# RWKV-7 block inversions for both token halves at once, on 64 partitions

## The chip, the cores and the metric

The kernel runs on one core of one Trainium2 chip. Its time is device microseconds from the first to the last instruction of one launch; the median of the runs counts. The engines of a core are TensorE (PE, with PEld for its weight loads), VectorE (DVE), ScalarE (ACT), GpSimd (POOL) and SyncE (SP). Each works through its own queue in order.

## What is computed

Two layers of a streaming encoder trunk on 512 tokens of width 1024, in float32. Layer 0 mixes tokens with two groups of heads: HGRN2 (four heads of 128) and RWKV-7 (eight heads of 64). Layer 1 mixes with an S5 group and four mLSTM heads. Behind each mixing stand an output projection and a SwiGLU feed-forward part. The change is in RWKV-7 alone:

```python
def step(state, inp):
    r_t, w_t, k_t, v_t, a_t, b_t = inp
    sa = jnp.einsum("bhvk,bhk->bhv", state, a_t)
    state = (state * w_t[:, :, None, :] + sa[..., None] * b_t[:, :, None, :]
             + v_t[..., None] * k_t[:, :, None, :])
    return state, jnp.einsum("bhvk,bhk->bhv", state, r_t)
```

Token by token this would be 512 steps. The kernel works in chunks of 64 tokens instead. Within a chunk each token's `sa` depends on those before it, which is a triangular system I - A of 64 x 64 per head and chunk. Its two diagonal blocks of 32 x 32 are inverted, and the rest is solved with matrix products.

## The kernel before

**Dense products.** A product with weights (`projg`, results in tiles named `d`) takes three TensorE matmuls per 128 x 128 block, because weights and activations are each split into a high and a low part. A product over 1024 features is 24 matmuls of 128 x 512. The split of the weights is a copy on ScalarE (`hi`, L369) and a subtraction (`lo`, L370) on VectorE, for a few units (`pu`) on GpSimd.

**RWKV-7.** Two heads make a pair, so there are pairs 0 to 3, and tokens are taken in two halves g = 0 and 1 of four chunks each. For pairs (2q, 2q+1), q = 0 or 1, there are three stages:

- `rwp(q, g)`: `rw_gates`, then `rw_prep` of both pairs side by side. It builds the matrices of each chunk. The products `r<-ar,bb` are masked into `pb` (L931), and their diagonal blocks go to DRAM (`scr_a`, L943) by DMAs of ScalarE's queue.
- `rw_inverse(q, g)`, written `inv`: GpSimd loads the 32 blocks of q and g from `scr_a` (L973), one block per partition (32 partitions x 1024 elements, tile `iu`), sets the diagonal (L974), and runs 30 steps of a multiply (L978, into `ti`) and an add (L980) in place. It then writes the result to `scr_u` (L982).
- `rwd(q, g)`: `rw_solve` of each pair loads the inverses from `scr_u` into the block-diagonal tile `ub` (L991, GpSimd's queue, four DMAs per pair) and solves with four products: `r<-y,ub`, `r<-z,amb`, `r<-z,ub`, `r<-pb,wu`, with `z` added on VectorE (L1004). Then `rw_chain` of both pairs carries the state from chunk to chunk and normalises the output (`bon`, L1068). The second half's chain needs the state that the first half's left (`hs`).

A pair of index p and p + 2 shares its tiles, and `ub` has one buffer for each of the two pairs of a q. So with q = 0 or 1 and g = 0 or 1 there are four inversions, each of 60 operations on GpSimd.

**HGRN2.** `hgrn(h)` does four dense products and then a head's chain on all engines; some of its subtractions (`e<-c`, L271) are GpSimd's.

**The order.** One stream `F` holds the dense products of the input projection in the order of `seq`: L (small gates), P0, P1 (projections of RWKV-7 pairs 0 and 1), H0 (HGRN2 head 0), P2, P3, H1, H2, H3. The table `prog` lists stages; each weaves a piece of `F`, up to the mark named, with other streams in proportion to costs that they yield (`m` scales them):

1. F to P1
2. `rwp(0,0)`, F to H0
3. `inv(0,0)`, `rwp(0,1)`, F to P2
4. `inv(0,1)`, `rwd(0,0)`, F to H1
5. `rwd(0,1)`, `rwp(1,0)`, F to H2
6. `inv(1,0)`, `rwp(1,1)`, F to H3
7. `inv(1,1)`, `rwd(1,0)`

Behind them `rwd(1,1)`, its costs scaled by 0.2, is woven with the first part of the output projection (`outa`: eight products of 15 matmuls, inputs `ysp`). The second part (L1226: 72 matmuls) needs RWKV-7's pairs 2 and 3 and head 3. A scheduler then orders the instructions of each engine by this order and by what is ready in its own estimate, so products written later can be drawn forward.

Of the kernel before, what the change touches and what calls it, by code (L numbers as in the profile page):

```python
# [10 lines left out]
F32 = mybir.dt.float32  # L11
# [75 lines left out]
def _cols(w, cols):  # L87
    """[K, N] -> [len(cols)/128, 128, K]: per column tile, k tiles side by side."""
    a = w[:, cols]
    k, n = a.shape  # L90
    a = a.reshape(k // P, P, n // P, P)
    return np.ascontiguousarray(a.transpose(2, 1, 0, 3).reshape(n // P, P, k))


def _rows(w, cols, per):
    """[K, N] -> [K/(128 per), 128, per N]: per k tiles side by side, all columns."""
# [6 lines left out]
def _layout(i):  # L103
# [78 lines left out]
    # S5: partitions hold (group of the pair, state), free dims the pair of groups  # L182
# [16 lines left out]
PRM = {'c': (0, 1, 2, 3), 'seq': ['L', 'P0', 'P1', 'H0', 'P2', 'P3', 'H1', 'H2', 'H3'], 'm': {'inv': 1.728, 'rwp': 1.6, 'rwd': 0.675}, 'prog': [[('F', 'P1')], [('rwp', 0, 0), ('F', 'H0')], [('inv', 0, 0), ('rwp', 0, 1), ('F', 'P2')], [('inv', 0, 1), ('rwd', 0, 0), ('F', 'H1')], [('rwd', 0, 1), ('rwp', 1, 0), ('F', 'H2')], [('inv', 1, 0), ('rwp', 1, 1), ('F', 'H3')], [('inv', 1, 1), ('rwd', 1, 0)]], 'e': 0.2, 'k': 8.0, 'dq': 'aggg', 'j': 0.9, 'eng': {('h8', 2): 'G', ('c5', 0, 0): 'S', 'h7': 'G', 'c7': 'S', ('p2', 3, 0): 'S', ('c1', 0, 0): 'S', ('c1', 1, 0): 'S', 'c6': 'V', 'c4': 'S', ('c1', 2, 0): 'V', 'h3': 'V', ('p14', 3, 0): 'V', ('h8', 1): 'G', ('c7', 1): 'V', ('c5', 1): 'V', 'h5': 'V', ('c8', 2): 'G', ('p2', 0): 'S', ('s4', 1, 0): 'S', 's2': 'S', 'c2': 'S', 'z1': 'G', 'z4': 'G', 'z6': 'G', ('z5', 0): 'V', ('a6', 3): 'G', 'p10': 'V', 'z9': 'V', 'p13': 'S', ('z2', 1): 'G', ('z0', 4): 'S', ('z1', 3): 'V', 'h13': 'V', ('a6', 2): 'G', ('z0', 1): 'G', ('h12', 1): 'V', ('n2', 2): 'V', ('p11', 1): 'S', ('a2', 2): 'V'}, 'pu': (2, 4, 5, 6, 7, 9, 12, 13, 36), 'i': 1.0, 'h': 0.7, 'f': 1.4, 'pr': {}}  # L199
# [3 lines left out]
def trunk(ctx: ExitStack, tc: tile.TileContext, A, out, dbg=None, start=0):  # L203
# [8 lines left out]
    class Pools:  # L212
        """pools that are opened one by one and closed together"""
# [25 lines left out]
    def act(o, i, f, bias=0.0, scale=1.0):  # L239
        """one table load for all the activations of a set that follow each other"""  # L240
# [11 lines left out]
    def sigmoid(o, x, nbias=0.0):  # L252
        """1 / (1 + exp(-x - bias)) by exp and ln alone"""
# [4 lines left out]
    def newton(r_, v, t):  # L258
        """one step towards r_ = v ** -0.5"""
# [17 lines left out]
    def ts(op, i, j, o, a, scale, bias, bias_s=None):  # L277
        """o = a * scale + bias"""
# [22 lines left out]
    # the weights in the order of their use, loaded and split ahead of it  # L301
# [29 lines left out]
    def wissue():  # L331
# [7 lines left out]
        if nm in NARROW:  # L339
            # both parts of few columns, side by side  # L340
# [26 lines left out]
    def split(h, l, src, eng=V):  # L367
        """src (SBUF, float32) = h + l"""
        S.copy(h, src)  # L369
        eng.tensor_tensor(l, src, h.bitcast(F32), SUB)  # L370
# [9 lines left out]
    def defer(f):  # L380
        """f after the next dense product; more banks until its result is there"""
# [29 lines left out]
    def run(gen, until=None):  # L411
        """advance a stream to its mark (or its end); its result"""
# [10 lines left out]
    def weave(*streams):  # L423
        """emit streams side by side, each up to its mark, in proportion to the costs that they yield"""
# [13 lines left out]
    def beside(*gens):  # L438
        """streams side by side as one stream"""
# [10 lines left out]
    class Norm:  # L450
        """hh + hl = x * gain, tile by tile; rstd = 1 / rms of x on all partitions"""
# [1285 lines left out]
```

## Time and profile before

| what | us |
|---|---|
| median of 3 runs | 1477.66 |
| lowest and highest run | 1477.18, 1478.99 |
| span of the profiled execution | 1480.0 |
| TensorE busy in it | 1423.6 (96%) |
| VectorE busy | 965.1 (65%) |
| ScalarE busy | 681.2 (46%) |
| GpSimd busy | 356.2 (24%) |
| the 240 operations of the four inversions (L978, L980) | 141.6 |

The profile shows one execution. A row of a timeline has the start in us from the start of the span, the time that it took, the engine, the line, the operation, the tiles (result <- inputs) and the shape. In brackets stands how long the engine stood idle ahead of it, and what ended that. A row of a group has a count, the busy time, the mean in ns of one, and the idle time ahead. A row of a stretch has its length and then each engine's busy time in it, the granted share of TensorE's clock, and DMA. Matmuls overlap in the pipeline, so a TensorE that reads busy is not always at its peak; the starts of its rows tell the rate.

### The profile page before, as it was taken

How to read it: one execution, taken by the hardware profiler on the slowest of the kernel's cores; microseconds unless marked ns; L12 is line 12 of the kernel's file. 1: busy time of each engine (PE TensorE's matmuls, PEld its weight loads, DVE VectorE, ACT ScalarE, POOL GpSimd, SP SyncE). 2: the span in 40 equal slices, each digit the busy share in tenths (PEclk: the TensorE clock that was granted, in tenths of full speed). 3: DMA queues.
4: the chain of work that ended last, by engine and by line, in shares of the span. 5: the costliest groups of instructions: out<-in, count | busy, mean ns of one | idle time of the engine just before them, and what ended most of it. 6: DMA issues, size and time to landing. Idle time of an engine off the chain costs nothing. (4 is left out here: it accounts for less than half of the span.)

```text
span 1480.0 us, 19897 instructions
## 1 busy us (share of the span) xinstructions
PE 1423.6 (96%) x6668; PEld 1140.6 (77%) x6668; DVE 965.1 (65%) x2035; ACT 681.2 (46%) x1594; POOL 356.2 (24%) x538
## 2 busy tenths in 40 slices
PE   8989999988999999999999899999999999999996
PEld 5777878767787888888888678766778888888885
DVE  7589669899688555555444677679785555554333
ACT  7554565645465333333333333477464343333332
POOL 5367740678320333110010542100020000000001
PEclk9989989998999999999999999999999999999998
DMA  5211221021323333333343832311233323323331
GB/s 186 86 36 46 63 71 50 30 56 47 116 84 100 108 102 102 106 97 105 104 128 100 208 107 80 113 57 29 64 102 92 100 89 97 100 86 96 91 109 62
DMA packets 51142, 133.39 MB, mean 90 GB/s; under 512 B 10640, under 2 KB 16272, under 8 KB 50784
## 3 DMA queue, kind: packets, MB, share of 16 engines
q1 hardware_dynamic: 38656, 116.86, 25.9%
q0 software_dynamic: 3024, 7.26, 2.0%
q10 hardware_dynamic: 9360, 8.00, 1.8%
q8 instruction: 53, 0.87, 0.2%
q14 instruction: 49, 0.40, 0.1%
HBM read 121.71 MB, written 10.39 MB: 89 GB/s over the span
## 5 line engine op out<-in xcount | busy, mean ns | idle before, releaser
L369 ACT CAST hi<-raw 128x256 fp32r<-128x256 f32 (+1 forms) x809 | 317.9, 402 | 528.7 <-PE d L286 480.1
L370 DVE TENSOR_TENSOR lo<-raw,hi 128x256 fp32r<-128x256 f32 (+1 forms) x774 | 348.0, 459 | 295.3 <-ACT hi L369 281.1
L286 PE MATMUL d<-hh,hi 128*128 128x512 f32 x1088 | 443.3, 407 | 2.9 <-DVE ur L1077 2.9
L286 PE MATMUL d<-hl,hi 128*128 128x512 f32 x1088 | 438.9, 403 | 0.0
L286 PE MATMUL d<-hh,lo 128*128 128x512 f32 x1088 | 438.9, 403 | 0.0
L286 PEld LDWEIGHTS d<-hh,hi 128*128 128x128 f32 x1088 | 208.4, 192 | 52.7 <-DVE ur L1077 3.4
L286 PEld LDWEIGHTS d<-hh,lo 128*128 128x128 f32 x1088 | 208.2, 191 | 49.0 <-issue 1.1
L286 PEld LDWEIGHTS d<-hl,hi 128*128 128x128 f32 x1088 | 208.2, 191 | 48.7 <-issue 2.4
L286 PE MATMUL d<-ah,hi 128*128 128x512 f32 x330 | 129.4, 392 | 0.0
L286 PE MATMUL d<-ah,lo 128*128 128x512 f32 x330 | 129.4, 392 | 0.0
L286 PE MATMUL d<-al,hi 128*128 128x512 f32 x330 | 129.4, 392 | 0.0
L1706 POOL TENSOR_TENSOR x<-x,f 128x256 f32<-128x256 f32 x6 | 5.2, 890 | 368.7 <-issue 362.2
L286 PE MATMUL d<-ysp,hi 128*128 128x512 f32 x224 | 74.1, 407 | 2.6 <-DVE x L1164 0.9
L467 POOL TENSOR_TENSOR rstd<-rstd,sq 128x512 f32<-128x512 f32 x21 | 28.6, 1363 | 193.9 <-ACT sq L247 183.7
L980 POOL TENSOR_TENSOR iu<-iu,ti 32x30 f32<-32x30 f32 (+14 forms) x120 | 71.3, 594 | 9.2
L286 PEld LDWEIGHTS d<-ah,hi 128*128 128x128 f32 x330 | 61.9, 188 | 14.0
L286 PEld LDWEIGHTS d<-al,hi 128*128 128x128 f32 x330 | 61.9, 188 | 13.9
L286 PEld LDWEIGHTS d<-ah,lo 128*128 128x128 f32 x330 | 61.9, 188 | 13.8
L978 POOL TENSOR_TENSOR ti<-iu 32x30 f32<-32x30 f32 (+14 forms) x120 | 70.3, 586 | 9.0
L286 PEld LDWEIGHTS d<-ysp,hi 128*128 128x128 f32 x224 | 41.2, 189 | 12.9 <-issue 1.9
L1187 DVE TENSOR_TENSOR g<-d,g 128x512 f32<-128x512 f32 x42 | 29.0, 691 | 27.5 <-PE d L286 27.5
L286 PE MATMUL d<-ysp,lo 128*128 128x512 f32 x112 | 45.5, 406 | 0.7 <-DVE lo L370 0.7
(489 smaller groups left out, 2046.1 us busy)
## 6 DMA issues: line engine op xcount, KB each, us to landing
raw<-in_wGU_dram SPq DMA_DIRECT2D x88, 512.0 KB, 3.6
raw<-in_wD_dram SPq DMA_DIRECT2D x32, 512.0 KB, 3.6
raw<-in_wA_dram SPq DMA_DIRECT2D x16, 512.0 KB, 3.6
raw<-in_wB_dram SPq DMA_DIRECT2D x13, 512.0 KB, 3.7
raw<-in_wD_dram SPq DMA_DIRECT2D x16, 384.0 KB, 3.1
raw<-in_wV_dram SPq DMA_DIRECT2D x6, 512.0 KB, 5.3
raw<-in_wQ_dram SPq DMA_DIRECT2D x6, 512.0 KB, 3.7
raw<-in_wK_dram SPq DMA_DIRECT2D x6, 512.0 KB, 3.6
```

Of the source, the lines that this page charges most:

```text
L286: T.matmul(o, w, a, start=start, stop=stop)
L369: S.copy(h, src)
L370: eng.tensor_tensor(l, src, h.bitcast(F32), SUB)
L467: self.eng.tensor_tensor(self.rstd, self.rstd, sq, ADD)
L978: G.tensor_tensor(t3, iu[:, j:j + 1, j + 1:].to_broadcast([32, j, n]), iu[:, 0:j, j:j + 1].to_broadcast([32, j, n]), MUL)
L980: G.tensor_tensor(iu[:, 0:j, j + 1:], iu[:, 0:j, j + 1:], t3, ADD)
L1187: V.tensor_tensor(g1, pu_, g1, MUL)
L1706: G.tensor_tensor(x[k][:, t], x[k][:, t], r_, MUL)
```

## The change

`rw_inverse` loses its argument g. It loads the 64 blocks of both halves on 64 partitions and runs the same 60 operations on them, so there are two inversions in place of four. The tile `iu` and the temporary `ti` grow from 32 to 64 partitions. DMAs of `scr_a` and `scr_u` move 256 KB in place of 128 KB. The stages are rearranged around it, since an inversion can only start when `rwp(q,0)` and `rwp(q,1)` are both done. `hgrn` gets a mark, H1a for head 1, behind its four dense products. Comments are taken out all over the file; the line numbers shift by one or two. The first piece of the diff is the value of `prog` in the parameter table.

```diff
-[[('F', 'P1')], [('rwp', 0, 0), ('F', 'H0')], [('inv', 0, 0), ('rwp', 0, 1), ('F', 'P2')],
- [('inv', 0, 1), ('rwd', 0, 0), ('F', 'H1')], [('rwd', 0, 1), ('rwp', 1, 0), ('F', 'H2')],
- [('inv', 1, 0), ('rwp', 1, 1), ('F', 'H3')], [('inv', 1, 1), ('rwd', 1, 0)]]
+[[('F', 'P1')], [('then', ('rwp', 0, 0), ('rwp', 0, 1)), ('F', 'H0')], [('inv', 0), ('F', 'H1a')],
+ [('rwd', 0, 0), ('F', 'H1')], [('beside', ('rwd', 0, 1), ('rwp', 1, 0))],
+ [('then', ('rwp', 1, 1), ('inv', 1)), ('F', 'H3')]]
...
                 V.tensor_tensor(u, ps, rstd, MUL)
                 us.append(u)
+            yield f"H{h}a"
             f, q, sg, vf = us
...
-        def rw_inverse(q, g):
+        def rw_inverse(q):
-            iu = pl.tile([32, 32, 32], F32, tag="iu", name="iu")
-            dq(1).dma_start(iu, scr_a[q, g].rearrange("p h b c s t -> (p h b c) s t"))
+            iu = pl.tile([64, 32, 32], F32, tag="iu", name="iu")
+            dq(1).dma_start(iu, scr_a[q].rearrange("g p h b c s t -> (g p h b c) s t"))
...
-                t3 = pl.tile([32, N2], F32, tag="ti", name="ti")[:, 0:j * n].rearrange("p (a b) -> p a b", b=n)
-                G.tensor_tensor(t3, iu[:, j:j + 1, j + 1:].to_broadcast([32, j, n]),
-                                iu[:, 0:j, j:j + 1].to_broadcast([32, j, n]), MUL)
+                t3 = pl.tile([64, N2], F32, tag="ti", name="ti")[:, 0:j * n].rearrange("p (a b) -> p a b", b=n)
+                G.tensor_tensor(t3, iu[:, j:j + 1, j + 1:].to_broadcast([64, j, n]),
+                                iu[:, 0:j, j:j + 1].to_broadcast([64, j, n]), MUL)
...
-            dq(2).dma_start(scr_u[q, g].rearrange("p h b c s t -> (p h b c) s t"), iu)
+            dq(2).dma_start(scr_u[q].rearrange("g p h b c s t -> (g p h b c) s t"), iu)
...
-        weave((scaled(rwd(1, 1), PRM.get("e", 1.0)), None), (outa(), "end"))
+        weave((scaled(build(("then", ("rwd", 1, 0), ("rwd", 1, 1))), PRM.get("e", 1.0)), None), (outa(), "end"))
```

`then` runs streams one after the other and `beside` runs them side by side; both were there already. How the scheduler's order moves is shown at three places. The numbers behind the names tell buffers apart.

**TensorE at the first solve of pairs 0 and 1** (`r<-y0,ub0`). Before, it stands between the transposes of `rw_prep` for the second half and the products of P3 (`d_1758`):

```order
L286 MATMUL d_1758<-hh_95,hi_1659 128x512
L962 MATMUL r_1565<-con_72,kb1_222 128x128 x4
L962 MATMUL r_1572<-con_72,bb1_218 128x128 x4
L286 MATMUL r_1579<-ek_1290,ak1_226 128x64 x4
L286 MATMUL d_1758<-hl_96,hi_1659 128x512
L286 MATMUL d_1758<-hh_95,lo_1660 128x512
L286 MATMUL r_1684<-y0_247,ub0_228 128x128 x4
```

Of the changed kernel the same solve follows on the last dense product of head 1 (`d_1918`), and behind it stand the transposes of that head (`m_1974`) and the first product of head 2 (`d_2688`):

```order
L286 MATMUL d_1918<-hh_95,hi_1863 128x512
L286 MATMUL d_1918<-hl_96,hi_1863 128x512
L286 MATMUL d_1918<-hh_95,lo_1864 128x512
L286 MATMUL r_2016<-y0_247,ub0_228 128x128 x4
L723 MATMUL m_1974<-con_72,vf_1952 128x128 x4
L286 MATMUL d_2688<-hh_95,hi_1902 128x512
```

Between the products `r<-ar3,bb1` of `rwp(0,1)` and this solve there now stand 168 dense matmuls, with no other stream among the last 165; before there were 20. From this solve to the same products of `rwp(1,1)` there are 192 dense matmuls where there were some 320.

**TensorE at the solve that follows on the last inversion.** Before, that is the second half's (`r<-y1,ub0`), with the first half's chain done just ahead of it and products of the output projection (`d_4290`) around it:

```order
L286 MATMUL r_3880<-kr2_264,con_72 128x256
L286 MATMUL d_4290<-ysp_3998,hi_4247 128x512
L286 MATMUL d_4290<-ysp_3999,hi_4247 128x512
L286 MATMUL r_3907<-la0_280,lora_147 128x256
L286 MATMUL r_4052<-y1_256,ub0_228 128x128 x4
L286 MATMUL d_4290<-ysp_3998,lo_4248 128x512
```

Of the changed kernel it is the first half's (`r<-y0,ub0`), among the second product of the output projection (`d_3837`) and the end of head 3 (`m_3554`, `m_3571`):

```order
L286 MATMUL m_3554<-u1_3306,st_3543 128x64
L286 MATMUL d_3696<-ysp_3670,lo_3373 128x512
L286 MATMUL d_3837<-ysp_3659,hi_3688 128x512
L286 MATMUL d_3837<-ysp_3658,lo_3689 128x512
L286 MATMUL r_3700<-y0_247,ub0_228 128x128
L286 MATMUL m_3571<-sq_3569,ones_76 128x512
L286 MATMUL r_3700<-y0_247,ub0_228 128x128 x3
L286 MATMUL d_3837<-ysp_3664,hi_3688 128x512
```

Ahead of it since `r<-ar3,bb1` stand the rest of `rwp(1,1)`, head 3 and 24 dense matmuls; behind it both halves' solves and chains and some 80 to 95 matmuls of the output projection's first part.

**GpSimd at the end of the last inversion.** Before, the loads of `ub` for the second half follow it, then one multiplication of a chain:

```order
L980 TENSOR_TENSOR iu_3710<-iu_3710,ti_3964 32x30
L982 DMA scr_u_209<-iu_3710 32x1024
L991 DMA ub0_228<-scr_u_209 32x4x32 x4
L991 DMA ub1_230<-scr_u_209 32x4x32 x4
L271 TENSOR_TENSOR kr0_246<-kr0_246,bon0_251 128x256
```

Of the changed kernel the loads of both halves follow it, the second of them into buffers that the first half's solve still reads:

```order
L982 TENSOR_TENSOR iu_3078<-iu_3078,ti_3609 64x29x2
L980 TENSOR_TENSOR ti_3612<-iu_3078 64x30
L982 TENSOR_TENSOR iu_3078<-iu_3078,ti_3612 64x30
L984 DMA scr_u_209<-iu_3078 64x1024
L993 DMA ub0_228<-scr_u_209 32x4x32 x4
L993 DMA ub1_230<-scr_u_209 32x4x32 x4
```

Five subtractions of HGRN2 head 3 (`e<-c`) now stand among the 60 operations of this inversion, where two did before.

More of the change, by code (lines that the diff above doesn't have):

```diff
@@ L196, in _layout @@
     return o
-PRM = {'c': (0, 1, 2, 3), 'seq': ['L', 'P0', 'P1', 'H0', 'P2', 'P3', 'H1', 'H2', 'H3'], 'm': {'inv': 1.728, 'rwp': 1.6, 'rwd': 0.675}, 'prog': [[('F', 'P1')], [('rwp', 0, 0), ('F', 'H0')], [('inv', 0, 0), ('rwp', 0, 1), ('F', 'P2')], [('inv', 0, 1), ('rwd', 0, 0), ('F', 'H1')], [('rwd', 0, 1), ('rwp', 1, 0), ('F', 'H2')], [('inv', 1, 0), ('rwp', 1, 1), ('F', 'H3')], [('inv', 1, 1), ('rwd', 1, 0)]], 'e': 0.2, 'k': 8.0, 'dq': 'aggg', 'j': 0.9, 'eng': {('h8', 2): 'G', ('c5', 0, 0): 'S', 'h7': 'G', 'c7': 'S', ('p2', 3, 0): 'S', ('c1', 0, 0): 'S', ('c1', 1, 0): 'S', 'c6': 'V', 'c4': 'S', ('c1', 2, 0): 'V', 'h3': 'V', ('p14', 3, 0): 'V', ('h8', 1): 'G', ('c7', 1): 'V', ('c5', 1): 'V', 'h5': 'V', ('c8', 2): 'G', ('p2', 0): 'S', ('s4', 1, 0): 'S', 's2': 'S', 'c2': 'S', 'z1': 'G', 'z4': 'G', 'z6': 'G', ('z5', 0): 'V', ('a6', 3): 'G', 'p10': 'V', 'z9': 'V', 'p13': 'S', ('z2', 1): 'G', ('z0', 4): 'S', ('z1', 3): 'V', 'h13': 'V', ('a6', 2): 'G', ('z0', 1): 'G', ('h12', 1): 'V', ('n2', 2): 'V', ('p11', 1): 'S', ('a2', 2): 'V'}, 'pu': (2, 4, 5, 6, 7, 9, 12, 13, 36), 'i': 1.0, 'h': 0.7, 'f': 1.4, 'pr': {}}
+PRM = {'c': (0, 1, 2, 3), 'seq': ['L', 'P0', 'P1', 'H0', 'P2', 'P3', 'H1', 'H2', 'H3'], 'm': {'inv': 1.728, 'rwp': 1.6, 'rwd': 0.675}, 'prog': [[('F', 'P1')], [('then', ('rwp', 0, 0), ('rwp', 0, 1)), ('F', 'H0')], [('inv', 0), ('F', 'H1a')], [('rwd', 0, 0), ('F', 'H1')], [('beside', ('rwd', 0, 1), ('rwp', 1, 0))], [('then', ('rwp', 1, 1), ('inv', 1)), ('F', 'H3')]], 'e': 0.2, 'k': 8.0, 'dq': 'aggg', 'j': 0.9, 'eng': {('h8', 2): 'G', ('c5', 0, 0): 'S', 'h7': 'G', 'c7': 'S', ('p2', 3, 0): 'S', ('c1', 0, 0): 'S', ('c1', 1, 0): 'S', 'c6': 'V', 'c4': 'S', ('c1', 2, 0): 'V', 'h3': 'V', ('p14', 3, 0): 'V', ('h8', 1): 'G', ('c7', 1): 'V', ('c5', 1): 'V', 'h5': 'V', ('c8', 2): 'G', ('p2', 0): 'S', ('s4', 1, 0): 'S', 's2': 'S', 'c2': 'S', 'z1': 'G', 'z4': 'G', 'z6': 'G', ('z5', 0): 'V', ('a6', 3): 'G', 'p10': 'V', 'z9': 'V', 'p13': 'S', ('z2', 1): 'G', ('z0', 4): 'S', ('z1', 3): 'V', 'h13': 'V', ('a6', 2): 'G', ('z0', 1): 'G', ('h12', 1): 'V', ('n2', 2): 'V', ('p11', 1): 'S', ('a2', 2): 'V'}, 'pu': (2, 4, 5, 6, 7, 9, 12, 13, 36), 'i': 1.0, 'h': 0.7, 'f': 1.4, 'pr': {}}
 @with_exitstack
```

## The prediction

> **What bounds the kernel now.** I read the slices of the page first, then the busy times by stretch, then single instructions at the points where the stretches meet.
>
> ```profile
> PE   8989999988999999999999899999999999999996
> DVE  7589669899688555555444677679785555554333
> PEclk9989989998999999999999999999999999999998
> ```
>
> Each digit is 37 us. Behind the twelfth slice TensorE stands at 9 with a full clock for some 400 us: dense products, which the change leaves alone. What can move is layer 0's mixing, slices three to twelve, where VectorE reads 8 or 9 and TensorE's clock drops below 9. So only 84 to 440 us is argued about. Its stretches, cut at the events quoted next:
>
> ```profile
> core 0: us, PE busy (x) PEld busy (x) DVE busy (x) ACT busy (x) POOL busy (x), PEclk, DMA share, GB/s
> 84.20:137.20 53.00, 47.01 (x256) 38.18 (x255) 47.63 (x93) 32.40 (x82) 42.58 (x70) 0.92 0.11 31
> 137.20:145.40 8.20, 8.20 (x46) 6.97 (x46) 6.93 (x18) 1.64 (x4) 4.36 (x8) 0.90 0.36 98
> 145.40:158.20 12.80, 12.73 (x88) 10.71 (x87) 9.51 (x29) 9.54 (x25) 3.37 (x11) 1.00 0.27 66
> 158.20:267.50 109.30, 106.89 (x595) 87.87 (x593) 83.23 (x183) 60.51 (x155) 45.63 (x77) 0.95 0.19 60
> 267.50:326.20 58.70, 54.95 (x297) 44.07 (x297) 55.54 (x123) 30.17 (x77) 45.48 (x75) 0.91 0.12 32
> 326.20:389.60 63.40, 53.57 (x345) 45.89 (x344) 52.96 (x111) 33.70 (x86) 44.53 (x76) 0.92 0.31 94
> 389.60:420.50 30.90, 29.52 (x175) 24.49 (x174) 19.77 (x44) 14.87 (x44) 3.55 (x5) 1.00 0.13 38
> ...
> 222.00:259.00 37.00, 36.67 (x219) 30.55 (x218) 33.75 (x82) 18.90 (x47) 0.00 (x0) 0.97 0.16 50
> ```
>
> VectorE fills 47.63 of 53.0 us in the first and 55.54 of 58.7 us in the fifth: it is the bound there, and GpSimd (the inversions) is busy beside it both times. In 222 to 259 us, GpSimd idle, VectorE still fills 33.75 of 37 us, or 91%.
>
> ```profile
> 145.44 0.68 DVE L931 TENSOR_TENSOR pb<-r,con 128x512 f32<-128x512 f32 x1
> 158.18 0.69 DVE L1004 TENSOR_TENSOR z<-y,r 128x512 f32<-128x512 f32 x1 [0.44 <-PE r L286]
> 326.18 0.68 DVE L931 TENSOR_TENSOR pb<-r,con 128x512 f32<-128x512 f32 x1
> 389.61 0.69 DVE L1004 TENSOR_TENSOR z<-y,r 128x512 f32<-128x512 f32 x1
> 420.47 0.41 DVE L1068 TENSOR_TENSOR bon<-kr,r 128x256 f32<-128x256 f32 x1
> ```
>
> These are: the last matrix that the inversion of pairs 0 and 1 needs (second half), the first solve of those pairs, the last matrix for pairs 2 and 3, the first solve of their second half, and the last output tile of RWKV-7.
>
> **The inversion itself.**
>
> ```profile
> 154.71 0.15 POOL L974 MEMSET iu<- 32x32 f32 x1 [4.45 <-DMA iu<-scr_a]
> 191.85 0.54 POOL L982 DMA_DIRECT2D scr_u<-iu  x1 [0.29 <-POOL iu L980]
> ...
> 335.40 0.30 POOL L974 MEMSET iu<- 32x32 f32 x1
> ...
> 377.24 0.54 POOL L982 DMA_DIRECT2D scr_u<-iu  x1 [0.29 <-POOL iu L980]
> ...
> L271 POOL TENSOR_TENSOR e<-c 128x256 f32<-128x256 f32 x30 | 21.0, 720 | 60.1 <-PE r L1040 49.2 <-PE m L722 5.9 <-DVE u L271 3.5
> L978 POOL TENSOR_TENSOR ti<-iu 32x240 f32<-32x240 f32 x8 | 6.2, 779 | 0.6
> ```
>
> One run of 60 operations takes 37.1 us (154.71 to 191.85), matrix to start 9.3 us (145.44 to 154.71). Two of the four runs go, some 74 us of GpSimd. What does an operation on 64 partitions cost? Nearest row: 128 partitions x 256 elements take 720 ns, 32 x 240 take 779 ns, so partitions cost nothing that this shows. I take 37.1 us for the doubled run; the other end is twice that, kept as a rival. The two DMAs move 256 KB instead of 128 KB; I count at most a microsecond, inside the ranges.
>
> **Where the time goes, step by step.** The new order has the same work before "last matrix of pairs 2 and 3" as the old one, but less behind which the inversions can hide. So I sum from event to event.
>
> *A. 84.2 to the last matrix of pairs 0 and 1 (61.2 us now).* The inversion that ran here leaves. What it costs VectorE:
>
> ```profile
> L370 DVE TENSOR_TENSOR lo<-raw,hi 128x256 fp32r<-128x256 f32 x7 | 4.6, 663 | 0.0
> L271 DVE TENSOR_TENSOR e<-e,k 128x256 f32<-128x256 f32 x6 | 4.3, 718 | 0.0
> L271 DVE TENSOR_TENSOR e<-e,u 128x256 f32<-128x256 f32 x6 | 4.2, 711 | 0.7 <-ACT e L247 0.7
> L271 DVE TENSOR_TENSOR e<-c 128x256 f32<-128x256 f32 x5 | 4.0, 809 | 0.0
> ...
> L370 DVE TENSOR_TENSOR lo<-raw,hi 128x256 fp32r<-128x256 f32 x16 | 6.1, 418 | 0.0
> L271 DVE TENSOR_TENSOR kb<-a,ek 64x256 f32<-64x256 f32 x4 | 1.7, 420 | 0.1
> ```
>
> The first four rows are 92 to 134 us, beside an inversion; the last two 222 to 260 us, without. The 24 instructions of the four groups took 17.1 us and would take 24 x 0.42 = 10.1 us: 7 us back, and I take 10 with the smaller groups. Two thirds of a dense product (16 matmuls) also stand later: 2 us. VectorE's 47.63 + 6.93 = 54.6 us become some 43; at 88% busy, **A is 49 us, -12**. Ends: 45 and 58.
>
> The Trainium skill, page "SBUF — State Buffer", section "Who interferes with whom", says that a VectorE instruction with two SBUF inputs contends with a GpSimd instruction that reads SBUF. The trace agrees: 663 against 418 ns for the same row. It speaks for the change, and carried to its end it is the second rival.
>
> *B. Last matrix to first solve (12.8 us now).* Today this solve needs the run of the first half alone, long finished by then. In the new order it needs the doubled run, which can't start before the last matrix. Chain: 9.3 to start, 37.1, then
>
> ```profile
> 386.39 1.06 PE L286 MATMUL r<-y,ub 128*128 128x128 f32 x8
> ...
> 154.92 1.05 PE L286 MATMUL r<-y,ub 128*128 128x128 f32 x8
> ...
> 69.12 0.40 PE L286 MATMUL d<-hh,lo 128*128 128x512 f32 x1
> 69.36 0.39 PE L286 MATMUL d<-hh,hi 128*128 128x512 f32 x1
> ```
>
> from store to solve 377.24 to 386.39, at most 9.2 us: 54 us taken, and 3.3 us to the z event (154.92 to 158.18). The cover is TensorE's: 168 dense matmuls, one every 0.233 us (69.12 to 69.36), are 39 us, with 7 us of small ones 46. So TensorE waits some 8 us at the first solve, and **B is 57 us, +44.5**. Ends: 49 (no wait) and 60. Queued behind that wait: the transposes of HGRN head 1, so VectorE runs dry too.
>
> *C. First solve to the last matrix of pairs 2 and 3 (168.0 us now).* The 168 dense matmuls of B came mostly out of here: 320 become 192. Two bounds. TensorE: 192 x 0.233 + 63 us of small products = 108 us. VectorE: 83.23 + 55.54 = 138.8 us now; 128 dense matmuls fewer are 5.3 products of four splits (0.42) and a 0.7 eviction or more, -14; without two inversions (some 73 us of GpSimd's 91; A gave 10 us back for 42.6) -15. That leaves 110 us, at the 91% of 222 to 259 us **C is 120 us, -48**. Ends: 108 and 132 (today's 83%).
>
> *D. Last matrix to the next solve (326.18 to 386.39, 60.2 us).* Today this wait belongs to the second half alone: the first half's inversion was finished, and its solve and chain filled the time. Now the solve of the **first** half waits for it. Length: 9.2 (326.18 to 335.40) + 37.1 + five e rows of HGRN head 3 set between its operations (3.6) + 9.2 = **59 us, -1**. Ends: 55 and 64. The cover: head 3 and 24 matmuls of the output projection, some 21 us of TensorE work. TensorE idles for over 25 us.
>
> *E. One more solve and chain behind it.*
>
> ```profile
> 413.36 0.67 PE L286 MATMUL r<-la,lora 96*128 96x256 f32 x2
> ...
> 438.72 0.39 PE L286 MATMUL d<-ysp,lo 128*128 128x512 f32 x1
> ```
>
> The second half's solve and chain, little beside it, run from 386.39 to 414.03 (413.36 + 0.67): 27.6 us. Now both halves stand behind the inversion, one after the other, since the second needs the first's state. **E is +27.6**. Ends: 24 and 33. Of the output projection some 95 matmuls (22 us) remain as cover, which only fills the chain's gaps.
>
> *F. Last tile to the end of the output projection (420.47 to 439.1, 18.6 us):* 64 of 72 matmuls are left, 15 us, and 2 us for the split: **17 us, -1.6**.
>
> *The clock.*
>
> ```profile
> 334.19 1.06 PE L950 MATMUL r<-con,raw 128*64 128x128 f32 x4 [4.55 <-ACT y L275]
> ...
> 333.40:343.60 10.20, 8.77 (x40) 8.24 (x41) 10.07 (x21) 7.65 (x20) 7.90 (x18) 0.50 0.00 1
> ```
>
> Behind a wait of 4.55 us the granted clock is 0.50 for 10 us. The idle stretch in D is longer and what follows is the solve, where TensorE sets the pace: **+4**, ends 0 and 7. The wait in B I count inside C's 91%.
>
> The Trainium skill, page "TensorE: Matmul & The Clock Gate", Part 1, gives the rule: about 3.4 us of idleness halve the clock until a busy window has passed. By it both new waits pay, as the row above shows; without it the sum would be 4 us lower.
>
> **Sum:** -12 + 44.5 - 48 - 1 + 27.6 - 1.6 + 4 = +13.5 us on the profiled 1480.0: 1493.5. Its span is 2.4 us over the runs' median of 1477.66, so **1491**. In short: gains of some 16 us ahead of the second inversion (A, B and C), given back in the tail.
>
> **Rivals.**
> *VectorE freed (not slower).* The place is C. If TensorE becomes its bound, C is 108 and A 45, and the freed tail brings E to 24 without the clock's 4: 13.5 - 12 - 4 - 3.6 - 4 = -10, that is 1467 to 1475. It decides from the point where A, C and E together come 13.5 us under what I took. For it: 663 against 418 ns. Against: heads 1, 2 and 3 and both second-pair preparations now stand there with 128 dense matmuls fewer to fill the gaps. 0.22.
> *No gain in the middle (slower still).* C keeps today's 83% and A loses only the 2 us moved: +12 and +10, 1513. For it: dependency waits within a head, which no freed engine shortens. Against: the fifth stretch already ran VectorE at 95%. 0.2.
> *The doubled run takes twice as long (the change doesn't halve anything).* +37 in B and +37 in D: 1565. Against: 720 ns on 128 partitions. 0.03.
> *Forecast as summed*, 1480 to 1502: 0.55.
>
> **Numbers.** 1491. Range 1472 to 1511: down into the first rival, up to the second, leaving out about 2 in 10. A difference below 0.2% (3 us) can't be told from none here. Faster 0.17 (most of the first rival), same 0.11 (its rest and the forecast's low edge), slower 0.72.
>
> **What would show it.** A: lo rows near 420 ns between 92 and 134 us, last matrix of pairs 0 and 1 near 133. B: TensorE waits for ub some 8 us near 180 to 187. C: last matrix of pairs 2 and 3 near 310. D and E: one wait of TensorE for ub, over 20 us, near 345 to 370, a clock of 0.50 behind it, and the last tile near 433. GpSimd's busy time falls by some 70 us. I am wrong if C ends before 300, or if no long wait stands ahead of the second inversion's solve.

## The result and the profile after

The changed kernel takes **1517.14 us** (median of 4 runs, 1511.45 to 1517.63) against 1478.33 for the kernel before beside it: a ratio of 1.0254, interval 1.0238 to 1.027. By the ratio it is slower by some 38 us where 13.5 were forecast, and it lies above the range. The profiled execution has a span of 1515.0 us, 35.0 more than before; its own steps are compared below.

The slices of the page after, as before:

```profile
PE   8999899977799999999999899999999999999996
DVE  7578668876468765555444579488895555554333
PEclk9999989995899999999999989899999999999998
```

A slice is 38 us now. TensorE has three in a row at 7 (303 to 417 us), and its clock reads 5 in the second of them. VectorE reads 7, 6 and 4 in these slices, where it read 9, 9 and 6 before (slices of 37 us): over these 114 us neither is full. The busy times by stretch, cut at the events of the prediction:

```profile
core 0: us, PE busy (x) PEld busy (x) DVE busy (x) ACT busy (x) POOL busy (x), PEclk, DMA share, GB/s
83.50:135.10 51.60, 47.96 (x274) 38.70 (x274) 40.27 (x102) 32.01 (x81) 5.05 (x7) 0.95 0.11 30
135.10:203.30 68.20, 57.27 (x277) 47.47 (x277) 43.60 (x83) 30.40 (x71) 45.89 (x79) 0.91 0.28 81
203.30:266.60 63.30, 62.52 (x395) 51.58 (x395) 53.04 (x129) 40.81 (x104) 10.17 (x17) 1.00 0.12 37
266.60:324.90 58.30, 54.97 (x329) 43.32 (x330) 49.09 (x128) 31.61 (x87) 2.54 (x4) 1.00 0.12 33
324.90:383.30 58.40, 35.91 (x173) 29.63 (x172) 36.19 (x67) 21.31 (x48) 43.41 (x76) 0.67 0.20 57
383.30:420.60 37.30, 31.57 (x174) 25.45 (x174) 18.36 (x42) 12.16 (x35) 6.79 (x13) 0.92 0.30 94
420.60:453.00 32.40, 31.45 (x190) 26.17 (x190) 21.86 (x52) 17.30 (x49) 1.62 (x2) 1.00 0.17 50
```

The second stretch (B) has TensorE idle for 11 of 68.2 us and the fifth (D) for 22.5 of 58.4. Both are the stretches in which GpSimd does a joint run. The two between them (C) are TensorE's: 117.5 of 121.6 us. The events themselves, in a timeline: last matrix, store of the inverses, first solve, its z; the same for pairs 2 and 3; the second half's solve and the last tile of RWKV-7.

```profile
135.09 0.69 DVE L932 TENSOR_TENSOR pb<-r,con 128x512 f32<-128x512 f32 x1
144.87 0.15 POOL L976 MEMSET iu<- 64x32 f32 x1 [4.63 <-DMA iu<-scr_a]
184.38 0.58 POOL L984 DMA_DIRECT2D scr_u<-iu  x1 [0.30 <-POOL iu L982]
192.73 0.55 PE L286 MATMUL r<-y,ub 128*128 128x128 f32 x1 [10.09 <-DMA ub<-scr_u]
203.33 0.69 DVE L1006 TENSOR_TENSOR z<-y,r 128x512 f32<-128x512 f32 x1
324.90 0.68 DVE L932 TENSOR_TENSOR pb<-r,con 128x512 f32<-128x512 f32 x1
333.10 0.15 POOL L976 MEMSET iu<- 64x32 f32 x1 [3.44 <-DMA iu<-scr_a]
376.10 0.59 POOL L984 DMA_DIRECT2D scr_u<-iu  x1 [0.30 <-POOL iu L982]
383.26 0.77 PE L286 MATMUL r<-y,ub 128*128 128x128 f32 x2 [8.30 <-DMA ub<-scr_u]
420.58 0.68 PE L286 MATMUL r<-y,ub 128*128 128x128 f32 x4
453.03 0.41 DVE L1070 TENSOR_TENSOR bon<-kr,r 128x256 f32<-128x256 f32 x1
```

Step by step, in us, with the last matmul of the output projection (end at 439.1 before, 470.9 after) closing the list:

| step | before | forecast | after | change forecast | change measured |
|---|---|---|---|---|---|
| A, to the last matrix of pairs 0, 1 | 61.2 | 49 | 50.9 | -12 | -10.4 |
| B, to the first z | 12.7 | 57 | 68.2 | +44.5 | +55.5 |
| C, to the last matrix of pairs 2, 3 | 168.0 | 120 | 121.6 | -48 | -46.4 |
| D, to the next solve | 60.2 | 59 | 58.4 | -1 | -1.9 |
| E, to the second half's solve, with the clock | 0 | 31.6 | 37.3 | +31.6 | +37.3 |
| second half's solve to the last tile | 34.1 | 34.1 | 32.4 | 0 | -1.6 |
| F, to the end of the projection | 18.6 | 17 | 17.9 | -1.6 | -0.8 |
| everything behind it | 1040.9 | 1040.9 | 1044.1 | 0 | +3.2 |
| sum | | | | +13.5 | +35.0 |

(A is counted from 84.2 in both, so its after is 135.09 - 84.2.) Of the events that the prediction named, the last matrix of pairs 2 and 3 came at 324.90 and not near 310, the last tile at 453.03 and not near 433, and the wait for `ub` in D was 8.30 us and not over 20.

### The profile page after: what moved, and what is told of

It reads as the page before. It is cut to its first block, busy times and chain, and to the rows that moved or that the text cites. A ratio compares the mean times of both kernels' runs of the same rounds, so it can differ in the third digit from the quotient of the medians.

```text
span 1515.0 us, 19759 instructions
## 1 busy us (share of the span) xinstructions
PE 1434.2 (95%) x6668; PEld 1143.2 (75%) x6668; DVE 949.9 (63%) x2035; ACT 683.5 (45%) x1594; POOL 282.5 (19%) x412
## 5 line engine op out<-in xcount | busy, mean ns | idle before, releaser
L286 PE MATMUL d<-ysp,hi 128*128 128x512 f32 x224 | 80.5, 432 | 12.1 <-ACT ysp L369 7.0
L1186 DVE TENSOR_TENSOR g<-d,rstd 128x512 f32<-128x512 f32 x42 | 29.0, 690 | 24.1 <-PE d L286 24.1
L370 POOL TENSOR_TENSOR lo<-raw,hi 128x256 fp32r<-128x256 f32 (+1 forms) x35 | 29.9, 865 | 67.4 <-ACT hi L369 43.5
```

The source lines that it names most:

```text
L286: T.matmul(o, w, a, start=start, stop=stop)
L1186: V.tensor_tensor(g1, pg, rstd, MUL)
```

## The experiments

### Each half of the change alone

One kernel has the joint run and the new order for pairs 0 and 1 and everything of before for pairs 2 and 3; the other the reverse. Only the table of stages, the tail and a choice between 32 and 64 partitions in `rw_inverse` differ. The diffs from here on are shortened to what matters:

```diff
 # joint for q = 0
+[('inv', 0), ('F', 'H1a')], [('rwd', 0, 0), ('F', 'H1')], [('rwd', 0, 1), ('rwp', 1, 0), ('F', 'H2')],
+[('inv', 1, 0), ('rwp', 1, 1), ('F', 'H3')], [('inv', 1, 1), ('rwd', 1, 0)]   # tail: rwd(1, 1)
 # joint for q = 1
+[('inv', 0, 0), ('rwp', 0, 1), ('F', 'P2')], [('inv', 0, 1), ('rwd', 0, 0), ('F', 'H1')],
+[('rwd', 0, 1), ('rwp', 1, 0), ('F', 'H2')], [('then', ('rwp', 1, 1), ('inv', 1)), ('F', 'H3')]   # tail: both halves
```

> One joint run on 64 partitions for pairs 0 and 1, in the changed order up to there; two runs on 32 partitions, with the stages and the tail of before, for pairs 2 and 3. Theory (the loss of the change is the tail: both halves' solves and chains stand behind the last inversion): the gains and losses around the first inversion about cancel, so -5 to +10 us against the kernel before, 1473 to 1488. The first solve still waits some 10 us for ub, the last solve is again the second half's. Rival (the loss is the wait for the first joint run, and what is dammed up behind it): +15 us or more, 1493 and up.

> The other half of the change alone: the order and the two runs of before for pairs 0 and 1, one joint run and the changed tail for pairs 2 and 3. Theory (the loss is the tail): +22 to +36 us against the kernel before, 1500 to 1514, with TensorE waiting for ub for more than 8 us ahead of the second inversion's solve and a granted clock of 0.50 about there. Rival (the loss is in the first half): within 10 us of the kernel before. If this and its counterpart add up to the whole change's +38, the two halves are independent.

Measured: 1.0121 (1.0106 to 1.0136), 1501.18 us, and 1.0166 (1.0148 to 1.0183), 1507.24 us, beside 1482.94. That is +18 and +24, together 42, where the whole change has 38: the halves are nearly independent. The second did as the theory said. The first did not: it fell to the rival. In the timelines, these are the last matrix of pairs 2 and 3 and the last matmul of the output projection, first of the kernel that is joint for pairs 0 and 1:

```profile
340.43 0.69 DVE L932 TENSOR_TENSOR pb<-r,con 128x512 f32<-128x512 f32 x1
454.65 0.39 PE L286 MATMUL d<-ysp,lo 128*128 128x512 f32 x1
```

and of the one that is joint for pairs 2 and 3:

```profile
316.81 0.68 DVE L932 TENSOR_TENSOR pb<-r,con 128x512 f32<-128x512 f32 x1
460.70 0.39 PE L286 MATMUL d<-ysp,lo 128*128 128x512 f32 x1
```

Before, these two stand at 326.18 and 438.72. Joint for pairs 2 and 3, the matrix comes 9.4 us earlier and the tail behind it is 143.9 us long in place of 112.5: the forecast's D, E, F and clock, +29, measured +31. Joint for pairs 0 and 1, the tail is 114.2 us, and 14.3 of the 18 us of loss lie ahead of the last matrix, where A, B and C were to bring a gain. That isn't the wait alone: C is 133.6 us there (206.80 to 340.43) against 121.6 in the change, and a run of pairs 2 and 3 (294.52 to 336.00) stands in it again.

### The runs cut short

The elimination loop stops after 2 steps in either kernel, and after 16 in the changed one:

```diff
-            for j in range(1, 31):
+            for j in range(1, 3):      # or range(1, 17)
```

> The changed kernel with 2 of the 30 elimination steps in each joint run, so the blocks' inverses are incomplete; all DMAs, stages and products stay. It takes some 69 us of GpSimd's time out. Theory (the loss is the time that the two runs stand on the path, B and the tail): 55 to 75 us less than the changed kernel, so 1440 to 1462, below the kernel before by 15 us or more; the two waits for ub fall under 2 us. Rival (the loss is the order itself: less dense work beside the small products, both chains in the tail, whatever the inversion takes): less than 35 us, so it stays above the kernel before.

> The kernel before with 2 of the 30 elimination steps in each of its four runs, so the blocks' inverses are incomplete; all DMAs, stages and products stay. It takes some 130 us of GpSimd's time out. Theory (the four runs slow VectorE beside them, and little of their length is on the path): 15 to 35 us less than the kernel before, 1443 to 1463, from VectorE's rows (lo at 663 ns beside a run going to some 420) and from the last run, whose wait in the tail goes. Rival (the runs are wholly hidden and disturb nobody): within 8 us of the kernel before.

> The changed kernel with 16 of the 30 elimination steps in each joint run, so the blocks' inverses are incomplete; all DMAs, stages and products stay. By the rows of the changed kernel a run is then some 24 us in place of 39 to 43, so 34 us of GpSimd's time go, where the kernel with 2 steps lost 78 us of it and 37 us of its time. Theory (what counts is how far a run reaches beyond the work that TensorE has beside it): the last 15 us of each run cost the most, the wait at the first solve is gone altogether, and 24 to 30 us are gained, 8 to 14 us above the kernel before. Rival (each microsecond of a run costs the same, by slowing the engines beside it): 34/78 of 37, 16 us gained, some 21 us above the kernel before.

Measured, as ratios to the kernel before:

| | 30 steps | 16 steps | 2 steps |
|---|---|---|---|
| stages of before | 1 | | 0.989 (0.9869 to 0.991) |
| stages of the change | 1.0254 (1.0238 to 1.027) | 1.0053 (1.0033 to 1.0072) | 1.0006 (0.9997 to 1.0016) |

Two things follow. The stages by themselves, with next to no run in either, cost 1.0006 against 0.989, or 17 us. So the theory put to the changed kernel with 2 steps (55 us or more) fell; it gained 37 us, just beyond the rival's 35, and came out level with the kernel before. The kernel before gained 16 us, the low end of its theory. And halving the GpSimd work made the inversions dearer, not cheaper: 37 us on the new stages, 16 us on the old ones. The 16-step kernel shows that this price isn't by the microsecond: the two runs took 82.5 us together; the first 36 us of them that go bring 30 us, the next 43 only 7. That is what the theory of reach said, and nearly twice what the rival allowed.

The two kernels with 2 steps have a blemish. In the profiled execution of either, TensorE's first matmul starts some 4 us later than in the other kernels (6.2 to 7.0 us), ahead of anything that was edited. Of the changed kernel with 2 steps:

```profile
11.01 0.79 PE L286 MATMUL r<-hh,hi 128*128 128x512 f32 x1 [11.01 <-ACT hi L369]
```

Why isn't shown. If it holds for their other executions too, either gain is some 4 us larger than it reads, 41 and 20, and the last 43 us of the runs are worth 11 and not 7. The 17 us between the stages stay, since both kernels have it. In the two kernels made from the change some 4 in 100 of TensorE's matmuls up to 480 us also stand elsewhere, since the scheduler reckons with shorter runs; in the one made from before its order is unchanged.

The busy times between the last matrix and the first matmul of the solve, for pairs 0 and 1 and for pairs 2 and 3, of the changed kernel:

```profile
135.09:192.73 57.64, 46.71 (x225) 37.99 (x224) 37.17 (x72) 24.83 (x59) 39.65 (x70) 0.94 0.33 94
324.90:383.26 58.36, 35.87 (x172) 29.59 (x172) 36.19 (x67) 21.31 (x48) 43.37 (x75) 0.67 0.20 57
```

of the one with 16 steps:

```profile
135.16:182.58 47.42, 46.65 (x225) 38.00 (x225) 32.01 (x69) 22.90 (x56) 25.10 (x43) 0.99 0.37 105
314.07:355.44 41.37, 27.17 (x138) 22.37 (x137) 28.04 (x56) 18.46 (x42) 27.80 (x48) 0.66 0.24 65
```

and of the one with 2:

```profile
141.28:188.76 47.48, 46.75 (x225) 38.09 (x224) 28.40 (x69) 22.88 (x56) 7.25 (x15) 0.98 0.35 105
320.24:340.98 20.74, 13.19 (x80) 10.64 (x79) 13.81 (x36) 14.30 (x35) 10.21 (x20) 0.75 0.38 104
```

The first row of each pair is the reading to learn: TensorE does the same 225 matmuls in the same 46.7 us in all three. With 16 or 2 steps they fill the stretch; with 30 it is 10.2 us longer than that. The forecast had taken 46 us for this cover. Once a run ends within it, more cutting buys nothing there. For pairs 2 and 3 the cover is short, so the price goes on: TensorE idles 22.5, 14.2 and 7.6 us. With 16 steps the first solve follows without a wait, and its z still comes 10.2 us later:

```profile
182.58 1.05 PE L286 MATMUL r<-y,ub 128*128 128x128 f32 x8
192.74 0.67 DVE L1006 TENSOR_TENSOR z<-y,r 128x512 f32<-128x512 f32 x1
```

### More cover, or a better place

Six edits of the changed kernel's order. First, the second run was to start earlier, with head 3 (or heads 2 and 3) behind it:

```diff
-[('beside', ('rwd', 0, 1), ('rwp', 1, 0))], [('then', ('rwp', 1, 1), ('inv', 1)), ('F', 'H3')]
 # inv1_early
+[('beside', ('rwd', 0, 1), ('rwp', 1, 0)), ('F', 'H2a')], [('rwp', 1, 1), ('F', 'H2')], [('inv', 1), ('F', 'H3')]
 # inv1_early2
+[('then', ('beside', ('rwd', 0, 1), ('rwp', 1, 0)), ('rwp', 1, 1))], [('inv', 1), ('F', 'H3')]
```

> The changed kernel with the second joint run moved forward: rwp(1,1) stands beside the chain of head 2 and the run beside head 3, instead of both beside heads 2 and 3 in a row. Theory (TensorE has no cover behind the second run): the wait for ub ahead of the second run's solve goes under 3 us and the half clock behind it goes, for which the stretches ahead of it get some of the time back; 12 to 28 us less than the changed kernel, 1492 to 1508. Rival (two chains in the tail and too little dense work beside the small products, wherever the run stands): within 8 us of the changed kernel, 1510 to 1525.

> As the one before, but both preparations of pairs 2 and 3 stand with no dense work beside them, so that heads 2 and 3 are all cover of the second run. Theory (cover): the wait for ub goes, and 10 to 30 us less than the changed kernel, 1490 to 1510. Rival (dense work taken from the preparations costs there what it brings behind): within 8 us of the changed kernel, with TensorE's busy share between 210 and 290 us below 0.93.

Measured: 1.0231 (1.021 to 1.0252) and 1.0264 (1.0247 to 1.0281). In number the rival's (though the sign that the second rival named didn't come: TensorE's busy share between 210 and 290 us is 0.99, not below 0.93), but the edits did not do what they were for. Of the first, the start of the second run:

```profile
333.35 0.15 POOL L976 MEMSET iu<- 64x32 f32 x1 [4.13 <-DMA iu<-scr_a]
```

That is 333.10 in the changed kernel. The run waits for its last matrix, at 324.47, whose preparation stands on VectorE behind the end of the first pairs' chain (305.02). The scheduler put things back: in the second kernel TensorE, ScalarE and GpSimd run the very order of the change, and VectorE's differs in four places of 2035; in the first, 20 of TensorE's 6668 matmuls stand elsewhere. So whether an earlier run would help was not tested. As a repeat of the change, the second tells how far a step can be trusted: A is 53.8 us in it for 50.9, B 66.5 for 68.2, C 121.6 for 121.6, E 39.0 for 37.3.

Then, more work ahead of the first solve: head 1 whole (`cover_h1`), or head 0 whole and head 1's dense products (`cover_h0`).

```diff
 # cover_h1
+[('inv', 0), ('F', 'H1')], [('rwd', 0, 0), ('F', 'H2a')], ...
 # cover_h0: seq is L, P0, P1, P2, P3, H0, H1, H2, H3
+[('then', ('rwp', 0, 0), ('rwp', 0, 1)), ('F', 'P3')], [('inv', 0), ('F', 'H1a')], ...
```

> The changed kernel with head 1 whole (its chain too) written ahead of the first solve, and the mark behind the dense products moved from head 1 to head 2. Theory (the wait at the first joint run holds up head 1's chain, which then stands in the solve's way, and the clock falls): y to z at the first solve takes some 4 us instead of 10.6, TensorE's idle time for ub there goes from 10 us to under 3, and the whole is 6 to 14 us less than the changed kernel, 1506 to 1514. Rival (the time to the first solve is the run's own length, and the work written behind fills it anyway): within 4 us of the changed kernel.

> The changed kernel with head 0 moved behind the projections of pairs 2 and 3 (seq is L, P0, P1, P2, P3, H0, H1, H2, H3), so that the first joint run has head 0 whole and head 1's dense products as its cover, and the preparations of pairs 0 and 1 have dense products alone beside them. Theory (cover): no wait for ub at the first solve, A shorter than now, since no head's chain stands beside the preparations on VectorE; 8 to 18 us less than the changed kernel, 1502 to 1512. Rival (head 0's chain slows head 1's products as much as the wait does): within 5 us of the changed kernel.

Measured: 1.0289 (1.0266 to 1.0313) and 1.0359 (1.0335 to 1.0383), the second clearly slower than the change, the first by some 5 us with intervals that just touch. Both theories missed, and the second's rival; the first's rival (within 4 us) is at its edge. In `cover_h1` the wait at the first solve went from 10.1 to 4.5 us and the one at the second from 8.3 to 21.3: cover for one run is taken from behind the other. With head 1 put ahead, the last matrix of pairs 2 and 3 came at 337.64 in place of 324.90.

Third, the order around either wait. `solve_first` writes the first solve ahead of head 1's chain; `tail_late2` writes the end of head 3 and five dense matmuls ahead of the solve that waits in the tail.

```diff
 # solve_first
-[('rwd', 0, 0), ('F', 'H1')]
+[('then', ('solve', 0, 0), ('solve', 0, 1))], [('beside', ('chain', 0, 0), ('chain', 0, 1)), ('F', 'H1')]
 # tail_late2: the stream of both halves yields 8.0 before it starts
+weave((late(8.0, scaled(build(("then", ("rwd", 1, 0), ("rwd", 1, 1))), 0.2)), None), (outa(), "end"))
```

> The changed kernel with the first solve of pairs 0 and 1 as a stage of its own, written ahead of head 1's chain, and the state chain woven with that head as before. Theory (of the 10.6 us from y to z at the first solve some 6 are head 1's work, which the wait dammed up and which stands ahead of z on ScalarE and VectorE): y to z takes 4 to 6 us, the last matrix of pairs 2 and 3 comes 3 to 6 us earlier, and the whole is 2 to 7 us less than the changed kernel. Rival (head 1's work is needed as soon, and is only put off): y to z shorter, but the last matrix within 2 us of now, and the whole within 2 us.

> The changed kernel with two and a half products of the output projection written ahead of the first half's solve in the tail, so that on TensorE the end of head 3 (m<-sq,ones) and five dense matmuls stand ahead of the waiting solve and not behind its first matmul. Theory (the wait for ub holds up head 3's end, the loads of x into head 3's memory, and with them the output projection): x is loaded 10 us or more before 397, no dense product waits for x, the segment from the solve to the second half's solve is 4 to 8 us shorter, and the whole 4 to 9 us less than the changed kernel. Rival (the two chains alone set the tail): within 3 us of the changed kernel.

Measured: 1.0283 (1.0269 to 1.0297) and 1.0252 (1.0238 to 1.0266). Of the first kernel, the solve, its z and the last matrix of pairs 2 and 3:

```profile
192.86 0.55 PE L286 MATMUL r<-y,ub 128*128 128x128 f32 x1 [6.70 <-DMA ub<-scr_u]
198.43 0.69 DVE L1006 TENSOR_TENSOR z<-y,r 128x512 f32<-128x512 f32 x1 [11.01 <-PE r L286]
326.33 0.68 DVE L932 TENSOR_TENSOR pb<-r,con 128x512 f32<-128x512 f32 x1
```

From y to z it takes 5.6 us in place of 10.6, as the theory said, but the last matrix is no earlier than 324.90: head 1's work was only put off. In the second, x was loaded at 395.82, 1.1 us earlier than the 396.93 of the change, the step from the solve to the second half's solve got longer (40.2 us for 37.3), and nothing was gained. Its rival holds. So does the first's as to the matrix, and the whole is 1.7 us slower than the change by the medians and 4 by the ratios, about its 2.

### The new stages with four runs

This one keeps the stages and the tail of the change but inverts each half on 32 partitions as soon as its own preparation is done:

```diff
-[('then', ('rwp', 0, 0), ('rwp', 0, 1)), ('F', 'H0')], [('inv', 0), ('F', 'H1a')]
+[('then', ('rwp', 0, 0), ('beside', ('rwp', 0, 1), ('inv', 0, 0))), ('F', 'H0')], [('inv', 0, 1), ('F', 'H1a')]
-[('then', ('rwp', 1, 1), ('inv', 1)), ('F', 'H3')]
+[('then', ('beside', ('rwp', 1, 1), ('inv', 1, 0)), ('inv', 1, 1)), ('F', 'H3')]
```

> The stages and the tail of the changed kernel, but four runs on 32 partitions: each half's run starts when its own preparation is done, the first half's beside the second half's preparation. The solves stay where the changed kernel has them, both halves behind the last run. Theory (the loss is that the first half must wait for the joint run, so that both chains stand behind it): the first half's solve of pairs 2 and 3 needs no wait and fills the wait of the second's; 15 to 30 us less than the changed kernel, 1488 to 1505, although GpSimd works 70 us more. Rival (the loss is the rearranged stages, whoever inverts): within 8 us of the changed kernel, 1510 to 1526.

Measured: 1.0184 (1.0168 to 1.0199), some 10 us less than the change: between the two. The row that tells why it isn't more is the first half's z:

```profile
369.13 0.68 DVE L1006 TENSOR_TENSOR z<-y,r 128x512 f32<-128x512 f32 x1
```

Its solve ran at 339.47, with no wait for `ub`, but z stands behind head 3's chain on VectorE. From the last matrix (330.95) to the end of the projection (462.07) it is 131.1 us, against 146.0 in the change and 112.9 before: of the tail's 33 us, 15 go when the first half need not wait for a joint run, and 18 stay with the rearranged stages. Another 6 us are lost ahead of it, since the last matrix comes at 330.95 for 324.90.

### The same runs, shorter

In step j the row that is multiplied by is still the original one, so the rows of a block can be worked on apart. With the rows of a block dealt out over two partitions (joint run, 64 blocks) or four (32 blocks), all 128 partitions work. In short form (t3 lies in rows of `iu` that are done with, and a step yields 0.6 in place of 1.2 to the weaving, so the order moves a little too):

```diff
+            for r in range(G):           # G = 2 joint, 4 split; m = 128 / G
+                iu[m*r : m*r+m] <- scr_a ; iv[m*r : m*r+m] <- rows r, r+G, .. of it
             for j in range(1, 31):
+                w = -(-j // G)
+                t3 <- iu[:, j, j+1:] * iv[:, 0:w, j]
+                iv[:, 0:w, j+1:] += t3
+            diagonal of iv = 1 ; scr_u rows r, r+G, .. <- iv[m*r : m*r+m]
```

> The changed kernel, nothing left out, with each of the 64 blocks on two partitions (even rows on one, odd rows on the other): the row that a step multiplies by is still the original one, so the rows of a block don't need each other, and an operation takes half the elements (at most 120 in place of 240). By the rows of the changed kernel (0.23 us at 30 elements, 0.44 at 150) a run is some 21 us in place of 39 to 43, and 2 to 4 us of DMA issues come on top. Theory (the reach of a run beyond TensorE's cover is what costs): as the kernel with 16 steps, 1484 to 1494, 5 to 16 us above the kernel before. Rival (the number of operations or the contention is what costs): 60 operations as ever, 1500 or more.

> The kernel before, nothing left out, with each of the 32 blocks of a run on four partitions (rows 0, 4, 8 .. on the first, and so on): at most 72 elements an operation in place of 240, a run of some 17 us in place of 37, with 4 us of DMA issues ahead and 2 us behind it. Theory (a run costs by the VectorE work beside it and by the wait in the tail): some half to two thirds of the 16 us that the kernel before gained with 2 steps, 1468 to 1475, faster than both kernels. Rival (the eight small loads and four stores of a run give it back): within 3 us of the kernel before.

Measured: 1.022 (1.0205 to 1.0236), 1510.71 us, and **0.9895 (0.987 to 0.992), 1461.08 us** beside 1478.66. The second is faster than both kernels, by 1% than the kernel before, and leaves nothing out. It gained nearly what the kernel before reads with 2 steps, more than the half to two thirds expected, although its runs take 23 to 29 us and not 17. The trace shows where: 16.9 of the 21.4 us between the profiled spans stand ahead of the last matrix of pairs 2 and 3 (309.25 for 326.18), so it is hardly the wait in the tail. And its runs slow VectorE less. Of the `lo` rows, 663 ns beside the first run of before and 418 with none, these are beside its own first run (99.6 to 126.2 us):

```profile
L370 DVE TENSOR_TENSOR lo<-raw,hi 128x256 fp32r<-128x256 f32 x8 | 3.6, 460 | 0.5 <-ACT hi L369 0.4
```

How much of the gain comes of this, how much of the shorter runs and how much of the moved order, wasn't told apart. The first kernel missed its number, since I had priced an operation by the quickest rows. The groups of the elimination (mean ns behind the comma), of the change:

```profile
L980 POOL TENSOR_TENSOR ti<-iu 64x30 f32<-64x30 f32 (+14 forms) x60 | 34.4, 574 | 4.3
```

of its stages with rows dealt out over two partitions:

```profile
L984 POOL TENSOR_TENSOR iv<-iv,iu 128x110 f32<-128x110 f32 (+20 forms) x60 | 26.2, 436 | 4.6
L982 POOL TENSOR_TENSOR iu<-iu,iv 128x110 f32<-128x110 f32 (+20 forms) x60 | 25.1, 418 | 7.7 <-DMA iv<-scr_a 3.3
```

and of the stages of before with rows over four:

```profile
L983 POOL TENSOR_TENSOR iv<-iv,iu 128x60 f32<-128x60 f32 (+10 forms) x120 | 44.7, 373 | 9.4
```

In the joint form it is 418 to 436 ns in place of 574: a run of 30 us, not 21, and with two loads and two stores the solve of pairs 0 and 1 comes 54.2 us behind the last matrix (137.07 to 191.25) in place of 57.6, that of pairs 2 and 3 55.9 (323.83 to 379.70) in place of 58.4. So 6 us less of reach gave 5 us. Its reach is close to the change's, and its time too; the rival's number holds, but not the rival's reason, as the 16-step kernel shows. The four kernels with these stages stand in the same order by the two stretches from last matrix to solve added up: 68.2, 88.8, 110.1 and 116.0 us go with +1, +8, +32 and +38 us. It is no straight line: the first 20.6 us more cost 7 (11 without the late start), the next 21.3 cost 24, the last 5.9 cost 6.

## Why the prediction was wrong

**A held.** -10.4 for -12. Of the VectorE rows between 92 and 134 us, beside which no inversion runs now, `lo` is at the 0.42 us that was taken, the others near it:

```profile
L271 DVE TENSOR_TENSOR e<-e,k 128x256 f32<-128x256 f32 x6 | 3.0, 494 | 0.0
L271 DVE TENSOR_TENSOR e<-c 128x256 f32<-128x256 f32 x5 | 2.3, 480 | 0.0
L370 DVE TENSOR_TENSOR lo<-raw,hi 128x256 fp32r<-128x256 f32 x5 | 2.0, 419 | 0.6 <-ACT hi L369 0.6
```

**The doubled run is one run.** 39.5 us (144.87 to 184.38) and 43.0 (333.10 to 376.10, with five `e` rows inside) against 37.1: 64 partitions cost what 32 do. GpSimd's busy time fell by 74 us, as said.

**B failed, by 11 us, half of the miss of 21.5.** "Last matrix to first solve: B is 57 us" became 68.2. Its mechanism was right (the solve waits for the joint run, and TensorE's cover is 46 us), and its terms were too small. From the matrix to the solve it is 57.6 us where 54 were taken (0.5 more in the start, 2.4 in the run, 1.6 by which 54 lay under its own terms, and 0.9 less in the loads of `ub`), and TensorE waits 10.1 us, not 8. From the solve to z it is 10.6 us where 3.3 were taken from before. That second term is not the wait: with 16 steps there is none, and from y (182.58) to z (192.74) it is still 10.2. It is head 1's chain, which the order puts ahead of z on ScalarE and VectorE. The prediction named what stands there ("queued behind that wait") and gave it no price in B, and it took none out of C. `solve_first` shows that B and C have to be read as one: 188.3 us there, 189.8 in the change (188.1 in its repeat), 177 in the forecast. With no wait at all, at 2 and at 16 steps, they are 179.0 and 178.9. So the forecast's 177 is about what B and C take with no wait, and the wait comes on top, 9 to 11 us. The forecast had 8 us of wait inside its 177: it priced the work itself at 169, 10 us too low, and the wait 1 to 3 us too low. Before, B and C took 180.7 us, so even with no wait the new order gains less than 2 there.

**C came out as the sum said, for another reason.** 121.6 for 120, so the first rival (VectorE freed) is out and the test "C ends before 300" was not met. But C was priced by VectorE, at 110 us busy, and VectorE was busy 102.1 us (53.04 + 49.09), while TensorE filled 117.5, though its own bound was put at 108. Those 108 held 63 us of small products for which no row was given; by the same working they were some 77 (117.5 less 176 dense matmuls at 0.233). So what the freed VectorE gave back was not the limit. The relief was also counted too high. In B and C together VectorE is busy 145.7 us, and was 148.3 before: 2.6 us back, not the 15 of the sum, which didn't charge the joint run in B (GpSimd busy 45.9 us there) beside VectorE's moved work.

**D held** (-1.9 for -1), as the run sets its length. TensorE is idle for 22.5 us where over 25 were said, but only 8.3 of them in one wait: the cover, put at 21 us of TensorE's work, kept it busy for 35.9, most of that at half clock.

**E was 5.7 us short.** One more solve and chain, with 4 us for the clock, measured 37.3 for 31.6. Two half-clock stretches stand there:

```profile
337.95:372.10 34.15, 25.24 (x97) 21.25 (x98) 27.55 (x42) 9.85 (x20) 31.40 (x46) 0.50 0.11 33
378.90:389.20 10.30, 5.94 (x18) 4.55 (x19) 1.12 (x2) 2.12 (x5) 4.37 (x8) 0.50 0.07 13
```

The clock falls not only behind the wait but for 34 us in D itself, where the run on GpSimd sets the length, and again as the solve begins, where it counts. The loads of x, at 396.93, hold up 25 dense matmuls (401.48 to 407.40) that then stand ahead of the chain; `tail_late2` didn't mend that, so how much of the 5.7 us each of the two has stays open.

**The sum.** A, B and C were to gain 15.5 us and gained 1.3. The tail was to lose 29 and lost 33. Another 3.2 us came behind the projection, on the same work, with five half-clock stretches of 27 us in all in place of 17; that the change causes it wasn't shown.

**The rivals.** "No gain in the middle" (1513) came nearest in number and says rightly where the gain failed to come, but not how: A gained, and C didn't come to the 132 us of VectorE at today's 83%. The wait for `ub`, and head 1's work ahead of z, ate what they brought. (Where the prediction speaks of 663 against 418 ns "carried to its end", it means the first rival that it lists, not the second.)

## What to carry to other kernels

Joining two runs of an engine that is off the critical path saves that engine's time and moves the start to the later of two inputs: price the stretch from the last input to the first use against the work that the bound engine still has in it, not the busy time saved. Where two stretches share a border at an event that the scheduler can put earlier or later, sum over both, since work that slips over the border is counted twice or not at all. If such a run has idle partitions, spread the same run over them and make it shorter in its old place: here that brought 1%, where moving it cost 2.5%.

## What the runs showed of the hardware

- An elementwise GpSimd operation gets cheaper by far less than its elements: on average 339 (multiply) and 373 ns (add) with at most 72 per partition (128 partitions), 418 and 436 with at most 128, 574 and 578 with at most 240 (64 partitions). From 32 to 64 partitions it costs nothing more: the 240 operations on 32 take 590 ns each (141.6 us), the 120 on 64 take 576.
- How much a GpSimd run slows VectorE beside it goes with the elements per partition and not with the count of partitions, as far as these runs tell. The `lo` subtraction takes 418 ns alone; 629 to 844 beside the runs on 32 partitions and 657 to 675 beside the joint ones (both at most 240 elements), 506 to 552 beside 128 partitions with at most 128, and 420 to 489 beside 128 partitions with at most 72.
- The Trainium skill, page "TensorE: Matmul & The Clock Gate", Part 1, lets the full clock return after one busy window of about 3.4 us. Here the granted clock stayed at 0.50 for 34.13 us from 337.95 on while TensorE read busy 25.24 of 34.15 us, so a TensorE that is busy three quarters of the time did not bring it back. It read busy for all of 348.19 to 351.60 and of 358.43 to 361.84, on bursts of 128x64 products mostly, and the clock did not come back behind either. (Busy by the profile isn't at its peak, so this shows only that a busy row isn't enough.)
